# Splitting the projection weights of two mixers ahead of time, during the feed-forward layers

## The chip, the cores and the metric

The kernel runs on one core of a Trainium2 chip. The metric is the device time of one execution in microseconds (us). The engines are named as in the profile: PE is TensorE (matrix products), PEld its weight loads, DVE is VectorE, ACT is ScalarE, POOL is GpSimd, SP is SyncE, which issues all DMAs of this kernel.

## The reference

Two blocks of two layers each over 512 tokens of 1024 features; the first block has 256 context tokens besides. All in float32.

```python
# first block, layers l = 0, 1
xl = xl + g1 * mixer_l(modulate(xl, ...))           # l = 0: gated linear attention + chunk MLP; l = 1: MLA + DFT
xl = xl + g2 * conv_ffn(modulate(xl, ...))          # up to 2 x 2816, convolution over 3 tokens, down to 1024
# second block
h = rms_norm(x) * (1 + scale) + shift
qa, ka, va, qb, kb, vb, g = split(h @ ab_w_in)      # first mixer: 8 dilated heads, 4 differential heads
x = x + gate * ((concat(ya, yb) * silu(g)) @ ab_w_out)
q, k, v, g = split(h @ c_w_in)                      # second mixer: 16 heads, 4 of keys and values, a band of 128
x = x + gate * ((y * silu(g)) @ c_w_out)
return rms_norm(x) * final_g
```

The modulation vectors (scale, shift, gate and so on) are products of a vector with matrices `ada_w` and `ada_w_2`; those matrices are read from DRAM too.

## The kernel before

Every product in float32 is made of three matmuls in the faster type float32r: an operand x is split into a high part H (x rounded to float32r) and a low part L = x - H, and the product is H H + L H + H L. The activations are split when they are made. The weights lie in DRAM as float32, packed in the order of their use as blocks of 128 partitions x up to 1024 columns (512 KB); a block serves 128 output features over 1024 input features (24 matmuls over 512 tokens), or half of the inputs for 256 output columns.

`Stream` carries them. `load` issues the DMA of the next block into a tile `raw` (line 71; `SLOTS` = 5 slots, shared with the matrices of the modulation vectors, which are loaded in line 242). `prep` makes a block's parts:

```python
nc.scalar.activation(h[:, :n], src, AF.Copy)                                    # line 85: wH
nc.vector.tensor_tensor(l[:, :n], src, h[:, :n].bitcast(F32), op=ALU.subtract)  # line 86: wL
```

Its tiles wH and wL have `HL` = 4 buffers each, and once a block has been split, the next raw load is issued, so that three raw blocks are loaded ahead. `take` hands a block to the product and first prepares the block behind it (`AHEAD` = 1; at the end of an output product 2). The products are `lin` (by features) and `lin_tm` (by tokens); all matmuls go through `mm`, line 333 in the profile.

The modulation vectors are made in steps spread over the products: a step takes a raw tile of 512 KB, ScalarE multiplies it (lines 304 and 308) and GpSimd adds it up (line 309); only then is its raw slot free. `run` emits such a step each time the counted time of TensorE has advanced by a set pace (9.2 us in the feed-forward layers, 11 us in the first mixer of the second block). A step's load is emitted together with its use.

The feed-forward layers are `ffn(0, ...)`, over 768 tokens, and `ffn(1, ...)`, over 512: three groups of hidden blocks, each an up product `up` and a down product `dn`. The first mixer of the second block is `even2`: it makes the keys, queries (`ab_kq`, 16 blocks), values (`ab_va`, `ab_vb`, 8) and gates (`ab_g`, 8) of 8 units (a unit is two dilated heads or one differential head with two softmaxes), and attends unit by unit; the products of unit i + 1 are emitted behind the attention of unit i and fill TensorE between its steps. The second mixer `odd2` does the same with `c_k` (2 blocks), `c_v` (2), `c_q` (8) and `c_g` (8). The output products `ab_out` and `c_out` follow. A scheduler at compile time sets the order of instructions on each engine by priority (the order of emission) and by when tiles come free; each engine, and SyncE's queue of DMA issues, works through its list in order.

Of the kernel before, what the change touches and what calls it, by code (L numbers as in the profile page):

```python
# [13 lines left out]
F32 = mybir.dt.float32  # L14
F32R = mybir.dt.float32r
U8 = mybir.dt.uint8
AF = mybir.ActivationFunctionType
ALU = mybir.AluOpType
# [29 lines left out]
class Stream:  # L48
    """Weight blocks in the order of their use, loaded ahead and split into two float32r parts."""

    def __init__(self, kk):
        self.kk = kk
        self.groups = []
        self.blocks = []
        self.loaded = self.prepped = self.used = 0
        self.raw = {}
        self.ready = {}

    def add(self, tag, ap, widths):
        g = len(self.groups)  # L60
        self.groups.append((ap, sum(widths)))
        o = 0
# [4 lines left out]
    def load(self):  # L67
        if self.loaded < len(self.groups):
# [6 lines left out]
    def prep(self):  # L75
# [3 lines left out]
        tag, g, o, n, last = self.blocks[self.prepped]  # L79
        while self.loaded <= g:  # L80
            self.load()
# [10 lines left out]

    def ahead(self, n):
# [3 lines left out]
    def take(self, tag, ahead=None):  # L97
        """The next block's parts; the blocks behind it are made ready first."""
# [4 lines left out]
        self.ahead(self.kk.AHEAD if ahead is None else ahead)  # L103
# [3 lines left out]
class Banks:  # L107
    """A product's token runs, each in a bank of PSUM that is taken when it is first named."""
# [14 lines left out]
class Kern:  # L123
# [5 lines left out]
    GLA_POOL = True  # L129

# [35 lines left out]
    def psum(self, parts, **banks):  # L166
        """Who takes which of the banks, in turn, from here on; parts: who, by part of the tokens."""
# [16 lines left out]

    def setup(self):
# [3 lines left out]
        self.ps = self.open("ps", space=bass.MemoryType.PSUM)  # L189
        self.psum(("mm", "mm", "aux"), mm=(0, 2, 1, 3), aux=(4, 6, 5))  # L190
# [43 lines left out]
    def ada_load(self, pool=None, bufs=0):  # L234
        """Step (m, b, n, k, d): of vector m the blocks of 128 columns b .. b + n, of its matrix the rows k .. k + d."""
# [16 lines left out]
    def ada_put(self, m, b, n, value, nv):  # L252
        """The modulation vector's blocks b .. b + n have their product: value."""
# [15 lines left out]
    def ada_pe(self, n):  # L269
        """The next n steps of modulation vectors, by TensorE."""  # L270
# [19 lines left out]
    def ada(self):  # L290
        """The modulation vectors: sums over the chunks of the rows by GpSimd, over the partitions by TensorE."""
# [1725 lines left out]
```

## Time and profile before

| | |
|---|---|
| median of 3 runs | 2305.15 us (2303.86 to 2305.77) |
| span of the profiled execution | 2305.6 us |
| TensorE busy | 2199.9 us (95%) |
| VectorE busy | 1542.2 us (67%) |
| ScalarE busy | 1118.7 us (49%) |
| GpSimd busy | 407.4 us (18%) |

The profiled execution has no time of its own beside its span; the span is 0.45 us over the median of the runs. In the profiled execution the first feed-forward layer runs from about 489 to 1050 us, the second from 1385 to 1712, the first mixer of the second block from there to about 2040, its output product to about 2067, and the second mixer to the end.

A row of busy time counts an engine's instructions; a busy TensorE is not a TensorE at its peak. "Idle" of a stretch is its length less the busy time. PEclk is the granted clock of TensorE as a share of full speed.

### The profile page before, as it was taken

To read this page: it belongs to the slowest core of one execution; us is meant where nothing else is said; L and a number is where in the kernel's file an instruction comes from. 1 tells how busy PE (TensorE), PEld (TensorE's weight loads), DVE (VectorE), ACT (ScalarE), POOL (GpSimd) and SP (SyncE) were. 2 spreads that over 40 slices of the span, in tenths; PEclk is the share of its full clock that TensorE was granted. 3 is DMA by queue.
4 is the path that set the end of the run, shared out by engine and by line. 5 is a ranking of instruction groups with operands and counts; after the bars stand their busy time and mean duration, and the time that the engine had idled before them with its cause. 6 is when DMAs were issued, how large, how long until landed. Compare 5 with 4: busy or idle time off the path is not lost.

```text
span 2305.6 us, 34273 instructions
## 1 busy us (share of the span) xinstructions
PE 2199.9 (95%) x13243; PEld 1880.2 (82%) x13243; DVE 1542.2 (67%) x2938; ACT 1118.7 (49%) x2124; POOL 407.4 (18%) x389
## 2 busy tenths in 40 slices
PE   6899899989999999999999999999999989989997
PEld 4788798788888888888889878878788877778886
DVE  5867775486545544547798675454567867968996
ACT  5444443254423423334577454343446756746773
POOL 0323321012122221221000013222211122101110
PEclk9999999999999999999999999999999999989999
DMA  9111111713333334331220134445434232213111
GB/s 322 65 47 32 33 56 38 283 56 125 106 117 110 113 107 128 105 115 59 76 92 1 46 119 138 145 131 155 137 108 137 80 95 92 73 56 95 56 46 37
DMA packets 86708, 226.78 MB, mean 98 GB/s; under 512 B 7184, under 2 KB 15376, under 8 KB 86544
## 3 DMA queue, kind: packets, MB, share of 16 engines
q1 hardware_dynamic: 86544, 224.58, 30.6%
q8 instruction: 104, 1.70, 0.3%
q14 instruction: 60, 0.49, 0.1%
HBM read 222.46 MB, written 2.10 MB: 97 GB/s over the span
## 4 chain that ended last, share of the span: by engine, by line
PE 75%; DVE 15%; ACT 5%; issue 2%; DMA 2%; POOL 1%; SPq 0%; DVEq 0%; ACTq 0%; POOLq 0%
PE b L333 72%; DVE wL L86 2%; DMA raw<-in_ada_w_dram 2%; DVE hL L463 1%; DVE n_t L461 1%; PE b L1130 1%; ACT wH L85 1%; PE b L280 1%; DVE s L1139 1%; DVE ptL L386 1%; PE b L1018 1%; DVE ksL L1092 1%; DVE n_acc L478 0%; PE b L316 0%; ACT ptH L385 0%
## 5 line engine op out<-in xcount | busy, mean ns | idle before, releaser
L333 PE MATMUL b<-hH,wH 128*128 128x256 f32 (+1 forms) x1880 | 597.6, 359 | 15.3 <-ACT hH L462 8.0
L333 PE MATMUL b<-hH,wL 128*128 128x256 f32 (+1 forms) x1880 | 593.5, 357 | 3.6 <-DVE wL L86 3.6
L333 PE MATMUL b<-hL,wH 128*128 128x256 f32 (+1 forms) x1880 | 588.9, 356 | 2.9 <-DVE hL L463 2.8
L309 POOL TENSOR_TENSOR gacc<-gacc,raw 128x512 f32<-128x512 f32 x182 | 261.5, 1437 | 1002.6 <-ACT raw L308 971.5
L333 PEld LDWEIGHTS b<-hH,wH 128*128 128x128 f32 x1880 | 356.0, 191 | 70.6 <-ACT hH L462 9.6
L333 PEld LDWEIGHTS b<-hH,wL 128*128 128x128 f32 x1880 | 357.6, 191 | 52.8 <-DVE wL L86 4.2
L333 PEld LDWEIGHTS b<-hL,wH 128*128 128x128 f32 x1880 | 355.5, 191 | 53.7 <-DVE hL L463 3.9
L86 DVE TENSOR_TENSOR wL<-raw,wH 128x1024 fp32r<-128x1024 f32 (+2 forms) x270 | 341.9, 1268 | 73.9 <-ACT wH L85 73.2
L85 ACT ACTIVATE wH<-raw 128x1024 fp32r<-128x1024 f32 (+2 forms) x270 | 278.1, 1031 | 176.0 <-PE b L333 173.4
L308 ACT ACTIVATE raw<-raw,csil 128x512 f32<-128x512 f32 x182 | 125.6, 717 | 202.4 <-DMA raw<-in_ada_w_dram 134.1
L333 PE MATMUL b<-hidH,wH 128*128 128x512 f32 (+1 forms) x563 | 167.8, 345 | 0.0
L333 PE MATMUL b<-hidH,wL 128*128 128x512 f32 (+1 forms) x563 | 167.4, 344 | 0.0
L333 PE MATMUL b<-hidL,wH 128*128 128x512 f32 (+1 forms) x563 | 167.2, 344 | 0.0
L333 PE MATMUL b<-yH,wH 128*128 128x256 f32 (+1 forms) x408 | 129.5, 334 | 5.1 <-ACT yH L385 4.9
L333 PE MATMUL b<-yH,wL 128*128 128x256 f32 (+1 forms) x408 | 129.5, 333 | 1.5 <-DVE wL L86 1.5
L333 PE MATMUL b<-yL,wH 128*128 128x256 f32 (+1 forms) x408 | 129.5, 334 | 0.0
L668 DVE TENSOR_SCALAR a<-gp,vecs 128x769 f32<-128x769 f32 (+1 forms) x44 | 39.1, 888 | 123.9 <-ACT gp L664 123.9
L333 PEld LDWEIGHTS b<-hidH,wH 128*128 128x128 f32 x563 | 105.5, 188 | 14.5 <-issue 1.2
L333 PEld LDWEIGHTS b<-hidH,wL 128*128 128x128 f32 x563 | 105.8, 188 | 13.6
L333 PEld LDWEIGHTS b<-hidL,wH 128*128 128x128 f32 x563 | 105.8, 188 | 13.1
L385 ACT ACTIVATE ptH<-b 128x384 fp32r<-128x384 f32 (+2 forms) x160 | 77.7, 500 | 64.7 <-PE b L1130 49.0
L333 PE MATMUL b<-wH,hH 128*128 128x256 f32 x352 | 100.9, 288 | 2.7 <-ACT z L519 1.5
(366 smaller groups left out, 3938.9 us busy)
## 6 DMA issues: line engine op xcount, KB each, us to landing
raw<-in_weights_dram SPq DMA_DIRECT2D x231, 512.0 KB, 3.5
raw<-in_ada_w_dram SPq DMA_DIRECT2D x144, 512.0 KB, 3.9
raw<-in_weights_dram SPq DMA_DIRECT2D x32, 448.0 KB, 3.3
x0t<-in_xT_dram SPq DMA_DIRECT2D x4, 768.0 KB, 7.0
xlat<-in_xT_dram SPq DMA_DIRECT2D x2, 1024.0 KB, 10.2
out_dram<-fo SPq DMA_DIRECT2D x8, 256.0 KB, 2.3
raw<-in_weights_dram SPq DMA_DIRECT2D x3, 384.0 KB, 3.0
xctx<-in_xT_dram SPq DMA_DIRECT2D x2, 512.0 KB, 7.0
```

Source lines behind the costliest of these rows:

```text
L85: nc.scalar.activation(h[:, :n], src, AF.Copy)
L86: nc.vector.tensor_tensor(l[:, :n], src, h[:, :n].bitcast(F32), op=ALU.subtract)
L280: nc.tensor.matmul(acc[32 * q:32 * q + 32, :], self.csil[:, k + a, :], raw[:, a, :, q, :], start=k + a == 0, stop=k + a == KD - 1)
L308: nc.scalar.activation(raw[:, a], raw[:, a], AF.Copy, scale=c)
L309: nc.gpsimd.tensor_tensor(acc[v], acc[v], raw[:, a], op=ALU.add)
L333: self.nc.tensor.matmul(ps, lhsT, rhs, start=start, stop=stop, **kw)
L385: self.nc.scalar.activation(h, src, AF.Copy)
L386: self.nc.vector.tensor_tensor(l, src, h.bitcast(F32), op=ALU.subtract)
L461: nc.vector.scalar_tensor_tensor(t, x(j, s, e), A[:, j, v:v + 1], r, op0=ALU.mult, op1=ALU.mult)
L463: nc.vector.scalar_tensor_tensor(hL[j][:, s:e], t, b, h.bitcast(F32), op0=ALU.add, op1=ALU.subtract)
L668: nc.vector.tensor_scalar(a, gp[:, 1:1 + L], cw(1, i), cb(i), op0=ALU.mult, op1=ALU.add)
L1018: nc.tensor.transpose(ps[:, c], P[:, a, c], self.ident)
```

## The change

The 32 blocks of `ab_kq`, `ab_va`, `ab_vb`, `ab_g` (tags `EARLY_EVEN`) are loaded and split during `ffn(0)`, the 20 blocks of `c_k`, `c_v`, `c_q`, `c_g` (`EARLY_ODD`) during `ffn(1)`, by a generator `make` that `run` advances by one block each time TensorE's counted time has grown by 13 us. Both parts are written to tiles in DRAM. In the mixers `prep` then loads the two parts by two DMAs straight into wH and wL instead of loading raw and splitting; `load` passes over these blocks, so the raw slots go to the blocks behind them; and `take` asks for two blocks ahead instead of one when the next block is such a one. `make` has a pool of its own, `early` (two raw tiles, two H, one L), that is closed before the last down product. The output weights and all other weights are split as before. Comments and docstrings are dropped as well.

```diff
     def load(self):
+        while self.loaded < len(self.groups) and self.split_before(self.loaded):
+            self.loaded += 1
         if self.loaded < len(self.groups):
...
     def prep(self):
...
         tag, g, o, n, last = self.blocks[self.prepped]
+        if self.split_before(g):
+            pair = []
+            for name, src in zip(("wH", "wL"), self.made.pop(self.prepped)):
+                pair.append(ring.tile([128, 1024], F32R, name=name, tag=name, bufs=self.kk.HL))
+                nc.sync.dma_start(pair[-1][:, :n].bitcast(F32), src)
+            self.ready[self.prepped] = pair
+            self.prepped += 1
+            return
...
+    def split_before(self, g):
+        return self.tags[g] in self.kk.EARLY
+
+    def make(self, tags, sbuf, dram):
+        nc = self.kk.nc
+        todo = [(i, *b) for i, b in enumerate(self.blocks) if b[0] in tags]
+        raw = []
+
+        def load(k):
+            if k < len(todo):
+                i, tag, g, o, n, _ = todo[k]
+                raw.append(sbuf.tile([128, 1024], F32, name="er", tag="er", bufs=2))
+                nc.sync.dma_start(raw[-1][:, :n], self.groups[g][0])
+
+        load(0)
+        for k, (i, tag, g, o, n, _) in enumerate(todo):
+            load(k + 1)
+            src = raw.pop(0)[:, :n]
+            h = sbuf.tile([128, 1024], F32R, name="eH", tag="eH", bufs=2)[:, :n]
+            l = sbuf.tile([128, 1024], F32R, name="eL", tag="eL", bufs=1)[:, :n]
+            nc.scalar.activation(h, src, AF.Copy)
+            nc.vector.tensor_tensor(l, src, h.bitcast(F32), op=ALU.subtract)
+            self.made[i] = [dram.tile([128, n], F32, name="ed%s%d" % (p, i)) for p in "HL"]
+            for d, t in zip(self.made[i], (h, l)):
+                nc.sync.dma_start(d, t.bitcast(F32))
+            yield
...
     def take(self, tag, ahead=None):
...
-        self.ahead(self.kk.AHEAD if ahead is None else ahead)
+        n = self.kk.AHEAD if ahead is None else ahead
+        if self.used < len(self.blocks) and self.split_before(self.blocks[self.used][1]):
+            n = max(n, self.kk.AHEAD_EARLY)
+        self.ahead(n)
         return self.ready.pop(i)
...
+    AHEAD_EARLY = 2
+    EARLY_EVEN = ("ab_kq", "ab_va", "ab_vb", "ab_g")
+    EARLY_ODD = ("c_k", "c_v", "c_q", "c_g")
+    EARLY = EARLY_EVEN + EARLY_ODD
...
     def run(self, *gens):
...
+                while self.pe >= self.make_next:
+                    next(self.make_gen, None)
+                    self.make_next = self.pe + self.make_every
...
     def ffn(self, l, T, segs, parts, n, x, nxt, side):
...
         self.ada_pace(9.2)
+        self.make_gen = self.W.make((self.EARLY_EVEN, self.EARLY_ODD)[l], self.open("early", n.side), self.dram)
+        self.make_every = (13.0, 13.0)[l]
+        self.make_next = self.pe + 6.0
...
             if last:
+                for _ in self.make_gen:
+                    pass
+                self.make_next = math.inf
+                self.close("early")
                 self.close(n.name)
```

## Rows read from the trace of the kernel before

**Rows 1.** The page: busy time by engine, and GB/s in 40 slices.

```profile
PE 2199.9 (95%) x13243; PEld 1880.2 (82%) x13243; DVE 1542.2 (67%) x2938; ACT 1118.7 (49%) x2124; POOL 407.4 (18%) x389
...
GB/s 322 65 47 32 33 56 38 283 56 125 106 117 110 113 107 128 105 115 59 76 92 1 46 119 138 145 131 155 137 108 137 80 95 92 73 56 95 56 46 37
```

**Rows 2.** Windows by stage: us, busy by engine (instructions), PEclk, DMA share, GB/s.

```profile
489.00:1050.00 561.00, 555.11 (x3343) 486.96 (x3342) 298.87 (x378) 206.75 (x302) 130.04 (x93) 0.99 0.35 111
1385.00:1712.00 327.00, 326.45 (x1477) 262.63 (x1475) 170.05 (x201) 131.43 (x182) 80.35 (x53) 1.00 0.46 139
1712.00:1745.00 33.00, 29.44 (x230) 28.45 (x230) 29.58 (x65) 20.66 (x43) 5.12 (x4) 0.95 0.38 120
1745.00:2000.00 255.00, 242.95 (x1255) 195.26 (x1256) 201.79 (x432) 174.22 (x337) 47.47 (x32) 0.99 0.30 94
...
2063.00:2100.00 37.00, 36.18 (x270) 33.71 (x269) 33.85 (x73) 23.76 (x50) 5.86 (x8) 1.00 0.26 78
2100.00:2240.00 140.00, 139.66 (x729) 113.61 (x727) 128.68 (x402) 101.93 (x281) 19.75 (x38) 1.00 0.21 65
```

**Rows 3.** Timeline of TensorE, 1800 to 1950: start, us, instruction, [idle before, releaser].

```profile
1833.85 0.63 PE L1130 MATMUL b<-ident,P 128*128 128x128 f32 x4 [0.58 <-DVE P L1287]
...
1839.07 0.63 PE L1130 MATMUL b<-ident,P 128*128 128x128 f32 x4 [0.87 <-DVE P L1287]
...
1865.91 0.75 PE L333 MATMUL b<-ksH,qs 128*128 128x512 f32 x1 [3.23 <-DVE sm L1139]
...
1888.08 0.66 PE L1130 MATMUL b<-ident,P 128*128 128x128 f32 x4 [1.06 <-DVE ptL L386]
...
1918.44 0.50 PE L333 MATMUL b<-ksH,qs 128*128 128x512 f32 x1 [0.92 <-DVE sm L1139]
...
1920.97 0.63 PE L1130 MATMUL b<-ident,P 128*128 128x128 f32 x4 [0.83 <-DVE P L1287]
```

**Rows 4.** Chain of waits, 1840 to 1915, in order of time: start us, us, what.

```profile
1850.17 5.67 DMA raw<-in_ada_w_dram
...
1860.06 2.23 DVE wL L86
...
1886.20 1.23 DVE wL L86
...
1911.82 3.58 DMA raw<-in_ada_w_dram
```

**Rows 5.** Groups of lines, 1745 to 2000: busy us, mean ns, idle before.

```profile
L86 DVE TENSOR_TENSOR wL<-raw,wH 128x1024 fp32r<-128x1024 f32 x29 | 37.7, 1301 | 3.9 <-ACT wH L85 3.8
...
L85 ACT ACTIVATE wH<-raw 128x1024 fp32r<-128x1024 f32 x30 | 31.5, 1051 | 0.6 <-PE b L333 0.5
```

**Rows 6.** Waits, 1745 to 2000: us in total, times, longest.

```profile
SPq L242 <- DVE wL L86: 94.7, 11, 26.7
...
ACT raw L308 <- DMA raw<-in_ada_w_dram: 10.4, 7, 3.3
```

**Rows 7.** Modulation matrices' loads, 1745 to 2000.

```profile
L242 SPq DMA_DIRECT2D raw<-in_ada_w_dram x16: 378/378/385, 1750.9 to 1977.8; - x16
...
DMA to landing us min/median/max: 3.5/3.7/5.7
```

**Rows 8.** Waits in the first feed-forward stretch, then in the second.

```profile
ACT wH L85 <- PE b L333: 45.6, 16, 7.3
...
PE b L333 <- DVE wL L86: 3.3, 1, 3.3
...
ACT wH L85 <- PE b L333: 76.8, 36, 4.4
```

**Rows 9.** Timeline of VectorE at the first boundary: start, us, instruction, [idle before].

```profile
1715.13 1.22 DVE L86 TENSOR_TENSOR wL<-raw,wH 128x1024 fp32r<-128x1024 f32 x1 [0.61 <-ACT wH L85]
```

**Rows 10.** Timeline of ScalarE and TensorE at the second boundary.

```profile
2063.50 1.05 ACT L85 ACTIVATE wH<-raw 128x1024 fp32r<-128x1024 f32 x1
...
2068.72 0.28 PE L333 MATMUL b<-hH,wH 128*128 128x256 f32 x1
```

More of the change, by code (lines that the diff above doesn't have):

```diff
@@ L53, in __init__ @@
         self.groups = []
+        self.tags = []
         self.blocks = []
@@ L57, in __init__ @@
         self.ready = {}
+        self.made = {}
     def add(self, tag, ap, widths):
@@ L61, in add @@
         self.groups.append((ap, sum(widths)))
+        self.tags.append(tag)
         o = 0
@@ L189, in setup @@
         self.ps = self.open("ps", space=bass.MemoryType.PSUM)
+        self.dram = self.open("dram", space=bass.MemoryType.DRAM)
+        self.make_gen, self.make_next = iter(()), math.inf
         self.psum(("mm", "mm", "aux"), mm=(0, 2, 1, 3), aux=(4, 6, 5))
@@ L463, in after @@
                 nc.vector.scalar_tensor_tensor(hL[j][:, s:e], t, b, h.bitcast(F32), op0=ALU.add, op1=ALU.subtract)
-        return SimpleNamespace(add=add, after=after, hH=hH, hL=hL, name=name, H=hHt)
+        return SimpleNamespace(add=add, after=after, hH=hH, hL=hL, name=name, side=side, H=hHt)
     def sumsq(self, pool, T, x):
```

## Prediction

> **What bounds the kernel now.** I read the page's busy line first, then the stretches by stage, then the gaps of TensorE inside the one stage where it has any to speak of, then the chain of waits and the waits of SyncE's queue there. The page shows TensorE busy 95% of the span, with VectorE at 67% and ScalarE at 49% [rows 1]: work taken from VectorE gains only where TensorE stands still for it. By stage [rows 2]: in the two feed-forward stretches TensorE is busy 555.1 of 561 us and 326.5 of 327 us, with VectorE at 53% and 52%. In the units of the second block's second mixer (2100 to 2240) it is busy 139.7 of 140, although VectorE is busy 92% there. The first mixer's stretch from 1745 to 2000 is another case: 243.0 of 255, so 12.05 us idle, with a granted clock of 0.99. So the place where these splits can cost time is that stretch, and little else: 1712 to 1745 has 3.6 us idle, 2063 to 2100 has 0.8. From 2000 on the first mixer ends with the last unit's own softmax and with output weights, which are still split in place.
>
> What ends the gaps between 1745 and 2000: six of them [rows 3] add up to 0.58 + 0.87 + 3.23 + 1.06 + 0.92 + 0.83 = 7.5 us, each released by VectorE. The chain of waits says what VectorE was late with [rows 4]: before the 3.23 us gap a modulation load was issued when a wL had freed its slot, ScalarE's multiplication of that load came 5.7 us later, and then two wL in a row (2.23 us) stood ahead of the statistics that release the score bank; before the 1.06 us gap stands one wL of 1.23 us. The waits show the same coupling in sum: SyncE's modulation loads waited 94.7 us for wL, and ScalarE, which works in order, stood 10.4 us in 7 waits for those loads [rows 6].
>
> **The change, part by part.**
>
> *Removed.* 52 splits: 16 + 8 + 8 blocks of the first mixer, 20 of the second. One costs 1301 ns on VectorE and 1051 ns on ScalarE [rows 5], together 68 and 55 us, which all move into the feed-forward layers. In 1745 to 2000 it is 29 wL (37.7 us of 201.8 busy) and 30 wH (31.5 of 174.2). What this buys on the path is bounded by nothing below (another link of the same chains takes the gap over) and by the whole 12.05 us above. I take the six gaps, 7.5 us, since before the two largest a wL is the link, and before the gap of 0.92 and the next a modulation load that came late [rows 4]. The clock: 0.99 over 255 us is about 2.6 us lost after pauses; I take half, 1.3.
>
> *Coupling of the loads.* Raw slots are no longer freed by wL: three stay with output weights that wait, two serve the modulation loads, freed by GpSimd's last addition. At one step per about 16 us (16 loads in that stretch [rows 7]) a load can be issued a step early, so ScalarE's 10.4 us of waits [rows 6] go. Their worth is inside the 7.5 us.
>
> *First boundary, 1712 to 1745.* The wL of 1.22 us at 1715.13 stands in VectorE's queue between the norm's steps [rows 9]; its block now comes by DMA. Two more follow in the norm's second half, while TensorE works. I take 1.0 us of gain; bounds 0 and the 3.6 us idle there.
>
> *Second boundary, 2063 to 2100.* The second of the first two key blocks gets its buffers when TensorE frees them at about 2063.5; today ScalarE then splits it at once, and the first matmul that needs it starts at 2068.72 [rows 10]. Now two loads of 512 KB run there. A load of 512 KB lands in 3.7 us [rows 7]; the second can land right behind the first or, at worst, a whole landing later, so the pair is there between 2067.2 and 2070.9: 0 to 2.2 us late. I take 0.5. The later key, value, query and gate blocks are asked for two ahead, which is at least one block of 48 half-width or 24 full-width matmuls before use: nothing.
>
> *Units of the second mixer, 2100 to 2240.* TensorE has 0.34 us idle: 0, though VectorE loses some 20 us of work. Tail from 2240: 0, its weights are unchanged.
>
> *Added in the feed-forward layers.* 32 and 20 times: one load, one ScalarE copy (1.05 us), one VectorE subtraction (about 1.2 to 1.3 us), two stores of 512 KB. VectorE goes from 298.9 to about 340 of 561 us and from 170.1 to about 196 of 327; ScalarE from 206.8 to 240 and from 131.4 to 152: room in sum [rows 2]. The cover is the depth of the weight preparation: ScalarE's wH waited for TensorE to free a buffer for 45.6 us in 16 waits in the first layer and 76.8 us in 36 in the second [rows 8], so it runs ahead of TensorE by all buffers there are, and a copy of 1.05 us or a wait behind it is absorbed. Without that cover each of the 52 would cost up to 2.3 us. It did fail in the first layer: TensorE stood 3.3 us for one wL [rows 8]. I take half of one more such stall, 1.5 us; bounds 0 and 6 (the first layer's waits, 5.9 us idle, once more). On SyncE's queue the two stores wait for ScalarE and VectorE, and the weight loads behind them wait along; three blocks are loaded ahead, so a wait of some us is hidden. Traffic in the second layer: 20 x 3 x 0.524 MB = 31.5 MB over 327 us are 96 GB/s on top of 139, so 235; the first slice of the page moved 322 [rows 1], so there is room, with longer landings. A store's landing is waited for by nobody until hundreds of us later.
>
> *Sum.* 2305.6 (span) - 7.5 - 1.3 - 1.0 + 0.5 + 1.5 = 2297.8. The profiled span lies 0.45 us above the median of the runs shown, 2305.15, so 2297.4.
>
> **A rule weighed.** The queue of SyncE is what the change lengthens: today its modulation loads already stood 94.7 us behind wL in 11 waits [rows 6]. The Trainium skill, "DMA: Bandwidth & Descriptors", section "Anatomy of one DMA", says that the DMA engines do not wait on semaphores; the wait is the issuing sequencer's, before it dispatches. By that rule a load of parts that waits for TensorE to free a wH buffer would hold every later load on the queue, and the trace agrees as far as SyncE's long waits go. What that would do here is the slower rival below.
>
> **The rivals.**
>
> *More is gained.* If the whole idle time of 1712 to 2000 goes (3.6 + 12.05), with 2.6 us of clock and no cost elsewhere: 2305.6 - 18.2 - 0.45 = 2287. For it: the second mixer's units keep TensorE at 139.7 of 140 us with VectorE at 92%, so VectorE at 64% (201.8 - 37.7 of 255) need not leave gaps. Against: the first mixer's chains are longer (a norm per unit, a second softmax).
>
> *The gaps only move.* ScalarE, the transposes' split and the softmax take over as the last link, so that 4 us are left of the gains, and the 2.0 us of costs (feed-forward layers and second boundary) stay: 2305.6 - 4 + 2.0 - 0.45 = 2303, up to no change. For it: five of the six gaps are released by the weighting of P or by the score statistics [rows 3], which stay on VectorE.
>
> *SyncE's queue holds ScalarE.* A load of parts stands at the head, waiting for TensorE to free a wH or wL, with a modulation load behind it; ScalarE, in order, waits for that load, and the softmax behind it. The place is 1745 to 2000, the price of one such case is the gap that the same chain makes today, 3.23 us. It decides from two on: 2305.6 + 2 x 3.23 + 2.0 (feed-forward and second boundary) - 1.0 - 0.45 = 2312.6. Against it: two slots let a modulation load go a step early, so the head must be held for more than some 12 us (16 less a landing of 3.7 [rows 7]).
>
> **How the numbers follow.** About 0.2% (4.6 us) is what a measurement of this kernel can tell from no change, so faster is below 2300.5 and slower above 2309.8. The forecast, 2290 to 2300, has 0.50; more gained 0.17; the gaps only move 0.20; the queue 0.13. That is faster 0.67, same 0.20, slower 0.13. The range for 8 in 10 takes the larger gain as far as 2285 and, on the other side, the moved gaps, no change and the milder cases of the queue up to 2308; the faster cases alone lie in 2285 to 2300.
>
> **What would show it.** After the change, TensorE's idle time in the first mixer's units should fall from 12 to about 4 us, with no wL on VectorE there, no wait of SyncE's modulation loads for wL, and ScalarE's waits for them near zero. The feed-forward stretches should keep their lengths within 1.5 us, with wH still waiting for TensorE. The second mixer's units should keep their length. The prediction is wrong if TensorE waits for DMAs into wH or wL by more than a few us in sum, if the feed-forward stretches grow, or if ScalarE's waits for modulation loads grow in place of vanishing.

## The result, and the profile after

The changed kernel takes 2339.8 us (median of 4 runs, 2335.9 to 2342.3) beside 2305.5 us for the kernel before: a ratio of 1.0142, 95% interval 1.0128 to 1.0157. The forecast was 2297.4 us, with a range up to 2308. The profiled execution of after is 2334.1 us long, 28.5 more than that of before; it is the fastest of the four runs, and the medians lie 34.4 us apart, so the stages below account for 28.5 of these.

Every trace here holds 13243 matmuls, so a stage can be cut by counting them (numbers 3497, 6913, 8463, 10226, 11982 and 12909 open the stages below; the last stage is taken up to the last matmul). Lengths of stages in us, worked out so from the two traces:

```
                             before    after   difference
first feed-forward layer      570.3    592.3    +22.0
its neighbour, second mixer   275.2    274.9     -0.3
second feed-forward layer     385.8    402.3    +16.5
2nd block: first mixer, out   349.1    337.7    -11.4
2nd block: second mixer       167.8    168.6     +0.8
output product, end            58.9     60.2     +1.3
```

The second block is 9.3 us shorter. The feed-forward layers, which were to keep their lengths, are 38.5 us longer. One cut is not quite the same in both kernels: around number 10226 the small matmuls that sum a modulation vector stand at other places in the order. Cut at the first product of the mixer instead, the second layer is 17.9 us longer and the second block 10.7 us shorter.

Line numbers differ between the runs, since each is that of the run's own kernel. First the page of after, its busy line and its traffic in 40 slices (compare [rows 1]):

```profile
PE 2203.3 (94%) x13243; PEld 1877.9 (80%) x13243; DVE 1547.7 (66%) x2938; ACT 1120.4 (48%) x2124; POOL 411.8 (18%) x389
...
GB/s 319 64 46 37 28 55 64 262 102 289 295 279 277 198 121 126 105 122 57 74 102 1 42 169 281 301 269 156 136 162 244 133 133 167 64 118 148 109 64 37
```

The busy times are those of before, within 6 us. The traffic is not: it stands at about 270 to 300 GB/s in slices 10 to 13 and 25 to 27 and then falls back, to between 105 and 160 for most of the rest of the layers. The last store of a block made ahead lands 295 us after the start of the first layer and 219 us after that of the second; the blocks are not spread over the layers. The waits of after in the first layer (488 to 1080), then in the second (1356 to 1759), from the views of waits (us in total, times, longest):

```profile
ACT raw L359 <- DMA raw<-in_ada_w_dram: 101.3, 22, 7.5
ACT eH L128 <- DMA er<-in_weights_dram: 58.7, 22, 8.2
DVE eL L129 <- DMA edL<-eL: 44.6, 15, 8.7
...
ACT wH L98 <- PE b L384: 20.9, 9, 5.5
...
ACT wH L98 <- PE b L384: 49.8, 23, 4.3
ACT raw L359 <- DMA raw<-in_ada_w_dram: 36.3, 17, 5.0
ACT eH L128 <- DMA er<-in_weights_dram: 30.4, 14, 6.5
DVE eL L129 <- DMA edL<-eL: 24.3, 9, 5.9
```

ScalarE stands 89 us for raw blocks that are to be split, VectorE 69 us for the store of the one eL buffer to land. ScalarE's waits for modulation loads are no longer than before in the first layer (101.3 beside 103.2 us in before) and longer in the second (36.3 beside 20.6). The slack of ScalarE ahead of TensorE, 45.6 and 76.8 us in [rows 8], is down to 20.9 and 49.8. The timeline of TensorE in after has seven gaps of 1.9 us or more among the products of the two layers that before does not have, and an eighth at the norm behind them; six of the seven (start, us, instruction, [idle before, releaser]):

```profile
620.01 1.28 PE L384 MATMUL b<-hH,wH 128*128 128x256 f32 x2 [2.81 <-ACT gp L718]
...
653.47 1.01 PE L384 MATMUL b<-hidL,wH 128*128 128x256 f32 x2 [5.21 <-DVE hidL L437]
...
727.48 0.35 PE L384 MATMUL b<-hH,wH 128*128 128x256 f32 x1 [2.53 <-DVE xctx L747]
...
1444.41 0.66 PE L367 MATMUL b<-gacc,ones 128*32 128x128 f32 x8 [3.36 <-ACT gp L718]
...
1492.39 0.47 PE L384 MATMUL b<-hidH,wH 128*128 128x512 f32 x1 [1.92 <-DVE gacc L369]
...
1538.72 0.66 PE L367 MATMUL b<-gacc,ones 128*32 128x128 f32 x8 [6.18 <-POOL gacc L360]
```

None waits for weights. TensorE waits for evacuations (gp, xctx), for hidden tiles (hidL) and for modulation sums (gacc): work that stands on ScalarE and VectorE behind something late. What was late ahead of the first two gaps is in the timelines of ScalarE and VectorE:

```profile
618.63 1.06 ACT L128 ACTIVATE eH<-er 128x1024 fp32r<-128x1024 f32 x1 [1.95 <-DMA er<-in_weights_dram]
619.60 0.85 ACT L718 ACTIVATE gp<-b 128x256 f32<-128x256 f32 x2
...
649.60 0.75 DVE L357 SCALAR_TENSOR_TENSOR gacc<-raw,csil,gacc 128x512 f32<-128x512 f32 x1 [4.89 <-DMA raw<-in_ada_w_dram]
```

At 620 us ScalarE had stood for a raw block, split it and only then evacuated gp. At 653 us VectorE had stood 4.89 us for a modulation load and made a wL before the hidL that TensorE needed. Ahead of the last gap, the timeline of SyncE's queue, ScalarE and GpSimd shows one modulation load and who waits for it:

```profile
1531.61 0.38 SPq L293 DMA_DIRECT2D raw<-in_ada_w_dram  x1
...
1536.00 0.72 ACT L355 ACTIVATE gacc<-raw,csil 128x512 f32<-128x512 f32 x1 [3.81 <-DMA raw<-in_ada_w_dram]
...
1537.41 1.28 POOL L360 TENSOR_TENSOR gacc<-gacc,raw 128x512 f32<-128x512 f32 x1 [5.83 <-ACT raw L359]
```

The granted clock falls at five of the seven gaps. Windows of after ahead of the first two gaps, right behind the second, and later (PE busy first, then PEld, DVE, ACT, POOL; PEclk, DMA share, GB/s):

```profile
545.00:600.00 55.00, 55.00 (x330) 48.19 (x330) 37.27 (x41) 28.38 (x38) 14.82 (x10) 1.00 0.87 292
```

```profile
653.50:657.50 4.00, 4.00 (x13) 3.42 (x14) 3.07 (x5) 2.17 (x3) 1.38 (x1) 0.50 0.71 253
658.00:700.00 42.00, 42.00 (x255) 36.68 (x254) 24.86 (x28) 14.29 (x17) 9.70 (x7) 1.00 0.83 294
```

At 292 GB/s TensorE runs without a pause at the full clock, and its matmuls keep the same 0.04 us behind those of before from 545 to 615 us, so traffic by itself does not slow matmuls here. The two gaps, 2.81 + 5.21 us, delay the matmuls around them by 5.0 + 8.2 us against before. Most of the difference is the clock: behind the second gap it is 0.50 of full speed, the lower of its two levels (1.2 GHz in place of 2.4), and 1.00 again from 658 us on. At the gaps of 727 and 1492 us (2.53 and 1.92 us) it stayed at 1.00, and the second of these delays the matmuls by 2.2 us only.

### The profile page after: what moved, and what is told of

Same layout as the page of the kernel before. It is cut to its first block, busy times and chain, and to the rows that moved or that the text cites. A ratio compares the mean times of both kernels' runs of the same rounds, so it can differ in the third digit from the quotient of the medians.

```text
span 2334.1 us, 34624 instructions
## 1 busy us (share of the span) xinstructions
PE 2203.3 (94%) x13243; PEld 1877.9 (80%) x13243; DVE 1547.7 (66%) x2938; ACT 1120.4 (48%) x2124; POOL 411.8 (18%) x389
## 4 chain that ended last, share of the span: by engine, by line
PE 61%; DVE 14%; DMA 10%; ACT 6%; issue 6%; POOL 3%; SPq 0%; DVEq 0%; ACTq 0%; POOLq 0%
PE b L384 58%; DMA raw<-in_ada_w_dram 5%; DMA edL<-eL 3%; DVE wL L99 2%; POOL gacc L360 2%; DMA er<-in_weights_dram 2%; DVE n_t L515 1%; PE b L1191 1%; DVE hL L517 1%; ACT wH L98 1%; ACT raw L359 1%; PE b L331 1%; PE b L1079 1%; DVE eL L129 0%; ACT P L1201 0%
## 5 line engine op out<-in xcount | busy, mean ns | idle before, releaser
L384 PE MATMUL b<-hH,wH 128*128 128x256 f32 (+1 forms) x1880 | 602.1, 361 | 26.3 <-ACT hH L516 10.7
L99 DVE TENSOR_TENSOR wL<-raw,wH 128x1024 fp32r<-128x1024 f32 (+4 forms) x218 | 276.2, 1269 | 76.9 <-ACT wH L98 76.5
L98 ACT ACTIVATE wH<-raw 128x1024 fp32r<-128x1024 f32 (+4 forms) x218 | 223.1, 1025 | 118.1 <-PE b L384 115.3
L129 DVE TENSOR_TENSOR eL<-er,eH 128x1024 fp32r<-128x1024 f32 x52 | 69.5, 1337 | 74.7 <-DMA edL<-eL 68.9
L437 DVE TENSOR_TENSOR ptL<-b,ptH 128x384 fp32r<-128x384 f32 (+2 forms) x160 | 89.0, 565 | 27.0 <-ACT ptH L436 25.5
```

Of the source, the lines that this page charges most:

```text
L129: nc.vector.tensor_tensor(l, src, h.bitcast(F32), op=ALU.subtract)
L384: self.nc.tensor.matmul(ps, lhsT, rhs, start=start, stop=stop, **kw)
L437: self.nc.vector.tensor_tensor(l, src, h.bitcast(F32), op=ALU.subtract)
```

## The experiments

Differences of stage lengths from before, in us, cut as above (columns: first feed-forward layer; second; second block's first mixer and output; the rest of that block), and the timed ratio to before on the same chip, with its interval. A stage comes from one profiled execution and scatters by some us; the ratio decides.

```
                 ffn 1   ffn 2   mixer   rest   ratio
after            +22.0   +16.5   -11.4   +2.1   1.0142 (1.0128 to 1.0157)
gain_alone        +4.5    +3.2    -8.5   +2.4   0.9974 (0.9960 to 0.9988)
cost_alone       +25.3   +18.1    -2.0   +0.2   1.0172 (1.0149 to 1.0195)
traffic_only     +14.9   +14.5    -7.6   +2.3   1.0099 (1.0074 to 1.0124)
no_stores        +17.0   +10.8    -8.8   +2.5   1.0102 (1.0081 to 1.0123)
paced            +13.2   +14.7   -11.6   +2.7   1.0090 (1.0064 to 1.0117)
after_late       +25.2   +20.5   -16.3   +2.2   1.0142 (1.0127 to 1.0157)
late              +9.7    +9.8   -17.4   +2.5   1.0021 (1.0008 to 1.0034)
gain_late         +1.2    +4.2   -16.0   +2.2   0.9976 (0.9965 to 0.9986)
before_late       +2.5    +1.0    -0.3   +0.1   1.0006 (0.9996 to 1.0015)
actq             +18.8   +21.4    -7.7   +2.5   1.0146 (1.0130 to 1.0163)
late_actq        +17.5   +13.2   -16.6   +2.3   1.0080 (1.0062 to 1.0098)
late_pre          +9.0    +3.6   -17.7   +2.2   1.0014 (1.0003 to 1.0026)
late_slow        +15.8    +5.2   -17.3   +2.2   1.0058 (1.0038 to 1.0077)
even_plain       +11.7   +17.7    -8.6   -0.2   1.0106 (1.0092 to 1.0119)
even_slow        +12.7    +3.0   -19.2    0.0   1.0020 (1.0009 to 1.0032)
even_late         +0.9    +8.8   -15.6   +0.2   0.9989 (0.9978 to 0.9999)
even_late13       +0.6    +5.2   -17.5   +0.1   0.9974 (0.9961 to 0.9986)
```

In the forms with the order edit (*late* below) eight modulation matmuls more fall into the mixer, so the cut by count moves. Cut at the first product of the mixer, the second layer and the mixer read +17.9 and -12.8 in after, +4.0 and -9.3 in gain_alone, +7.5 and -15.1 in late, +1.9 and -13.8 in gain_late, -1.3 and +2.0 in before_late, +3.0 and -15.2 in even_late13: up to some 3 us of these two columns hang on the cut.

**Gain and cost apart.** *gain_alone*:

```diff
+        every, todo = todo, todo[:1]
...
+            for j, *_ in every:
+                self.made[j] = self.made[i]
```

> Leaves out all but the first of the splits made ahead in each feed-forward layer; the 52 blocks of the second block load that one pair of parts again and again, so the loads of parts keep their size, number and place, and the output is that of other weights. Theory (the whole loss lies in the feed-forward layers and the second block alone gains 11.7 us): 2305.5 - 11.7 = 2294, between 2291 and 2297, feed-forward layers 570 and 385 us long as before. Rival (the second block is only shorter because work was pushed out of it into the longer feed-forward layers, modulation steps above all): 2300 to 2306.

*cost_alone*:

```diff
-        return self.tags[g] in self.kk.EARLY
+        return False
```

> The splits ahead are made and stored as in the change, but nothing reads them: the second block loads raw blocks and splits them in place as before. Theory (the loss is that of making them, and comes whether they are used or not): 2305.5 + 40 = 2345, between 2340 and 2350, feed-forward layers 592 and 403 us long. Rival (part of the loss comes from the loads behind: the weight stream skips the early groups, so that its ring holds other blocks in the feed-forward layers): 2325 to 2338.

The cost comes whether the parts are used or not (1.0172; median 2350.0, at the upper end of what was expected). The gain alone is 0.26%, some 6 us beside that chip's 2309.5, about half of the 11.7 expected and inside the rival's range; the second block is 6.1 us shorter here beside 9.3 in after. (Most of the +4.5 us of its first layer is one wait at the start of the layer, 5.74 us for the norm's hL at 516 us, 1.59 us in before; why stays open. The profiled execution is 4.8 us slower than the median.)

What the rival names can be counted. The loads of modulation matrices in the second layer, in before and then in after:

```profile
L242 SPq DMA_DIRECT2D raw<-in_ada_w_dram x34: 378/379/379, 1344.2 to 1712.1; - x34
```

```profile
L293 SPq DMA_DIRECT2D raw<-in_ada_w_dram x38: 367/379/480, 1366.0 to 1753.0; - x38
```

Every form that loads parts in the mixers has 38 to 40 there, and 10 to 12 in the first mixer; before, before_late and cost_alone, which load none, have 34 and 16. So modulation work did move out of the mixer into the second layer. It has a price at the layer's end, where TensorE waits for the sums of squares of the norm (n_acc). Before, then ScalarE (n_sq are the squares) and TensorE in after:

```profile
1712.36 0.70 PE L333 MATMUL b<-n_acc,ones 128*128 128x256 f32 x2 [0.91 <-DVE n_acc L478]
```

```profile
1749.49 1.33 ACT L359 ACTIVATE raw<-raw,csil 128x512 f32<-128x512 f32 x2 [1.38 <-DMA raw<-in_ada_w_dram]
1750.72 0.40 ACT L531 ACTIVATE n_sq<-xlat 128x256 f32<-128x256 f32 x1
...
1751.94 0.70 PE L384 MATMUL b<-n_acc,ones 128*128 128x256 f32 x2 [2.96 <-DVE n_acc L532]
```

The wait is 0.9 us in before, before_late and cost_alone and 2.1 to 4.2 us in every form that loads parts, gain_alone (3.30) and gain_late (3.16) among them. This part of the loss is not that of making parts.

**Traffic or work.** *traffic_only* stores the raw tile twice, from three raw buffers in place of two:

```diff
-                raw.append(sbuf.tile([128, 1024], F32, name="er", tag="er", bufs=2))
+                raw.append(sbuf.tile([128, 1024], F32, name="er", tag="er", bufs=3))
...
-            nc.scalar.activation(h, src, AF.Copy)
-            nc.vector.tensor_tensor(l, src, h.bitcast(F32), op=ALU.subtract)
...
-            for d, t in zip(self.made[i], (h, l)):
-                nc.sync.dma_start(d, t.bitcast(F32))
+            for d, t in zip(self.made[i], (src, src)):
+                nc.sync.dma_start(d, t)
```

> Keeps every load and both stores of the 52 blocks, but takes the copy off ScalarE and the subtraction off VectorE: the raw block is stored twice, so the low part is wrong. Theory (the in-order engines stand for the loads and stores of the blocks, 89 us on ScalarE and 69 us on VectorE by the waits, and TensorE behind them): most of the 40 us goes, 2294 to 2304, feed-forward layers at most 8 us longer than before together. Rival 1 (the traffic itself, 280 to 300 GB/s, makes weights and modulation rows late): 2325 to 2340. Rival 2 (only the engines' work of 2.3 us a block costs): 2292 to 2296, no trace of the traffic at all.

*no_stores*:

```diff
-            for d, t in zip(self.made[i], (h, l)):
-                nc.sync.dma_start(d, t.bitcast(F32))
+            if k == 0:
+                pair = [dram.tile([128, n], F32, name="ed%s%d" % (p, i)) for p in "HL"]
+                for d, t in zip(pair, (h, l)):
+                    nc.sync.dma_start(d, t.bitcast(F32))
+            self.made[i] = pair
```

> The change as it was, unpaced, but only the first block of each layer is stored; the others are loaded and split and dropped, and the second block loads that one pair each time, so the output is that of other weights. Engine work is that of the change, extra bytes in the feed-forward layers a third of it. Theory (what is waited for is DMA: landings of the raw block on ScalarE, of the store on VectorE, of the modulation rows): of 22.0 and 18.2 us at least half goes, 576 to 582 and 389 to 395, ratio 0.999 to 1.005. Rival (engine work of 2.3 us a block): 588 to 592 and 400 to 403, ratio 1.012 to 1.015.

Both theories fell as sole causes. Without any split, 29.4 of 38.5 us stay; without two thirds of the extra bytes, 27.8 stay. The two add up to more than the whole. That fits a TensorE that stands only for the last of several late things, each kind of delay being enough; no run shows this by itself. Where TensorE stands differs. The timeline of traffic_only has the modulation sum in the second layer; that of no_stores the evacuation behind ScalarE's copies:

```profile
1530.00 0.66 PE L363 MATMUL b<-gacc,ones 128*32 128x128 f32 x8 [6.43 <-POOL gacc L356]
```

```profile
1443.11 0.66 PE L369 MATMUL b<-gacc,ones 128*32 128x128 f32 x8 [7.14 <-ACT gp L720]
```

How long modulation loads take beside this traffic is in the views of their lines, in the second layer of before (137 GB/s) and then in after, 1400 to 1571 (284 GB/s):

```profile
DMA to landing us min/median/max: 3.5/3.7/5.4
```

```profile
DMA to landing us min/median/max: 4.3/5.7/7.8
```

In the first layer the median goes from 3.8 to 4.3 us only.

**Pace and order.** *paced* ties each load and each copy to real progress:

```diff
+        def pace(t):
+            if self.kk.pace is not None:
+                nc.vector.tensor_scalar(t[:, :1], self.kk.pace, 1.0, None, op0=ALU.mult)
...
+                pace(raw[-1])
...
+            pace(h)
...
+                    self.pace = hf[:, :1]
...
+                    self.pace = x(b, s, e)[:, :1]
```

> The change, with two tiny VectorE operations more per block: one element column of the raw buffer and one of the high part's buffer is first written from the newest hidden or residual tile, so that neither the load nor the copy can run ahead of the feed-forward layer's own progress; the real values overwrite them. Theory (the loss comes from running ahead: all blocks are made in the first 300 us of 570 and 170 us of 385, in a burst of DMA on whose landings ScalarE and VectorE stand): feed-forward layers within 4 us of 570 and 385, total 2294 to 2302, below the kernel before. Rival (the work costs what it costs, 52 times a copy and a subtraction on engines that release TensorE): 2330 to 2340 whatever the pace.

The forecast of the theory failed (1.009), though most of the waits it spoke of went. The view of waits of paced, first layer (44.6 and 58.7 us in after):

```profile
DVE eL L135 <- DMA edL<-eL: 13.5, 4, 4.6
ACT eH L134 <- DMA er<-in_weights_dram: 5.5, 2, 5.2
```

and what TensorE stands for in its second layer:

```profile
1435.27 0.43 PE L373 MATMUL b<-gacc,ones 128*32 128x128 f32 x8 [3.64 <-ACT gp L724]
...
1658.60 0.65 PE L373 MATMUL b<-gacc,ones 128*32 128x128 f32 x8 [6.88 <-POOL gacc L366]
```

ScalarE's slack ahead of TensorE is back at 43.7 us in the first layer (20.9 in after, 45.6 in before). So a second theory: the modulation chain (load, ScalarE, GpSimd) runs behind its place in the order, and TensorE meets it there. *late* is paced with the sums 5 us later in TensorE's order; *after_late* and *before_late* have this edit alone on the two kernels, *gain_late* on gain_alone:

```diff
             if k + d == KD:
+                yield "late"
                 nv = len(acc)
...
-                    next(self.ada_gen, None)
-                    self.ada_next = self.pe + self.ada_every
+                    due = self.pe + self.ada_every - self.ada_lag
+                    self.ada_lag = 5.0 if next(self.ada_gen, None) == "late" else 0.0
+                    self.ada_next = self.pe + self.ada_lag if self.ada_lag else due
```

> The paced form, and the small matmuls that sum a finished modulation vector over the partitions stand 5 us of TensorE's time later in the order than its last addition. Theory 1 (the rest of the loss comes from modulation loads that land late, so that TensorE, in order, stands for GpSimd's last addition: 3.64 and 6.88 us in the second layer, 13 us with what follows each): second layer 386 to 391 us in place of 400.5, first layer about as paced, 583; ratio to before 1.002 to 1.005. Theory 2 (it is not that wait but bytes or engine work everywhere): second layer stays at 398 to 402, ratio 1.008 to 1.010.

> The change as it was, unpaced, with the small matmuls of a finished modulation vector 5 us later in TensorE's order. If the late modulation vectors were the whole loss: ratio to before 1.001 to 1.004, as paced and later together. If running ahead is a cost of its own (ScalarE and VectorE standing for the landings of raw blocks and stores, 5.0 and 8.2 us of delay near 620 to 670 us, which no matmul of a modulation vector stands in): 1.005 to 1.010.

> The kernel before with nothing but the later matmuls: the control. It has no wait of TensorE for a modulation vector in the feed-forward layers, so the edit should give nothing there: ratio 0.998 to 1.001. If it gives 0.996 or less, part of what the paced and later form won was won by the edit and not for the change.

> Only the first block of each layer made, all loads of parts kept (output of other weights), with the later matmuls. This is what the change would be worth if making the parts cost nothing. Theory (no cost in the feed-forward layers, second block 8 to 17 us shorter): ratio 0.991 to 0.996, feed-forward layers 570 to 575 and 385 to 389 us. Rival (the shorter second block of the paced and later form, 331.8 us, came from modulation steps done in its longer feed-forward layers): 0.996 to 0.999.

The pair of edits takes 1.0142 to 1.0021. Pace alone gives 1.009, order alone nothing (1.0142), which is above both ranges expected of it: unpaced, the waits only change places, as the timeline of after_late shows:

```profile
1539.82 0.43 PE L369 MATMUL b<-gacc,ones 128*32 128x128 f32 x8 [3.02 <-POOL gacc L361]
...
1591.72 0.66 PE L369 MATMUL b<-gacc,ones 128*32 128x128 f32 x8 [4.06 <-ACT gp L721]
```

The ratio of late is in theory 1's range; its second layer, 395.7 us, lies between the ranges of the two theories. The control before_late is no faster (1.0006). gain_late, 0.9976, is within the rival's range, above what the theory gave: all that this change was worth with the cost of making parts taken away is about 0.25%. The gap that late keeps is again ScalarE in order, behind a modulation load; its timeline, then the windows behind it:

```profile
1007.36 1.33 ACT L366 ACTIVATE raw<-raw,csil 128x512 f32<-128x512 f32 x2 [3.36 <-DMA raw<-in_ada_w_dram]
...
1009.44 0.83 ACT L444 ACTIVATE hidH<-hf 128x768 fp32r<-128x768 f32 x1
...
1010.32 1.01 PE L392 MATMUL b<-hidH,wH 128*128 128x256 f32 x2 [4.76 <-ACT hidH L444]
```

```profile
1010.00:1015.50 5.50, 4.46 (x13) 3.46 (x14) 4.83 (x7) 2.02 (x4) 0.82 (x1) 0.50 0.54 171
1016.00:1035.00 19.00, 19.00 (x111) 16.73 (x110) 7.50 (x10) 6.12 (x10) 6.14 (x4) 1.00 0.28 91
```

A gap of 4.76 us costs 8.1 us against the same matmuls of before: the granted clock is at its lower level, 0.50, up to 1015.50 and at 1.00 from 1016 on.

**SyncE's queue.** *actq*, and *late_actq* with the order edit (the blocks are made in half steps of 6.5 us, with a third one-column write each):

```diff
-                nc.sync.dma_start(raw[-1][:, :n], self.groups[g][0])
+                nc.scalar.dma_start(t[:, :n], self.groups[g][0])
...
+            yield
+            pace(l, l[:, :1].bitcast(F32))
...
-                nc.sync.dma_start(d, t.bitcast(F32))
+                nc.scalar.dma_start(d, t.bitcast(F32))
```

> The paced form with the loads and stores of the blocks that are made on ScalarE's DMA queue in place of SyncE's, the stores half a step behind the subtraction. Bytes and engine work stay. Theory 1 (SyncE's queue, in order, stands for the copy, the subtraction and the pace operations, about 95 us more in the first layer, and holds modulation and weight loads behind): first layer 570 to 576, second 385 to 391, ratio 0.996 to 1.001. Theory 2 (the DMA engines are shared, and loads land 0.5 to 1.2 us later whatever queue they come from): 580 to 584 and 397 to 401, ratio 1.007 to 1.010, with ScalarE's waits for modulation loads as long as in the paced form (144 and 78 us).

> Both edits together. If each cures what its theory says: 570 to 574 and 384 to 388, ratio 0.995 to 0.999, below the kernel before. If the bytes cost it whatever the order: not below 1.004.

This theory fell: 1.0146 and 1.0080, slower by 0.6% than the same forms on SyncE's queue. The waits for modulation loads are as long as before the move; in the first layer of actq they are

```profile
ACT raw L376 <- DMA raw<-in_ada_w_dram: 94.3, 21, 10.1
...
DVE gacc L374 <- DMA raw<-in_ada_w_dram: 38.9, 15, 5.8
ACT gacc L372 <- DMA raw<-in_ada_w_dram: 37.5, 8, 9.7
```

which is 171 us, beside 166 in paced. It was 172 in the kernel before, though, so this sum does not tell the forms apart. What made actq slower than paced was not settled; the half steps and the third write are not told apart from the queue.

**Loads ahead, spacing, number.** *late_pre* loads one modulation step ahead, *late_slow* spaces its blocks by 16.0 and 17.5 us:

```diff
+            if self.ada_loaded <= self.ada_used:
+                self.ada_load()
             if k + d == KD:
```

> The paced and later form, with each modulation load issued one step (9.2 us of TensorE's time) ahead of its use. Theory (what is late is the modulation load, issued when its step comes and landing 4 to 5 us after, with ScalarE in order behind it, 135 us of such waits in the first layer): those waits fall below 60 us, the last large gap (4.76 us, ScalarE's copy of the hidden tile) goes, feed-forward layers 570 to 576 and 385 to 391 us, ratio 0.994 to 1.000. Rival (the load ahead takes a slot from the weight blocks, and weights come late in its place): 1.002 to 1.008.

> The paced form with later matmuls and loads ahead, blocks spaced 16.0 and 17.5 us in place of 13. Theory (the cost goes with the rate at which blocks are made): the gap of 3.58 us before the last product of the first layer may stay, the rest of the 8 us goes, first layer 572 to 577, second 386 to 389, ratio 0.997 to 1.000. Rival (each block costs the same however spread): ratio 1.001 to 1.003.

Neither did what it was for. In late_pre ScalarE still stands 122 us for modulation loads in the first layer (112 in late), and the ratio differs from that of late by less than the intervals; the wider spacing was slower (1.0058), with 7.77 us of idle TensorE at the same place, 1018 us, where blocks were still being made. The control, *before_late_pre*, is the kernel before with these loads and the order edit:

> The kernel before with the later matmuls and the modulation loads one step ahead, nothing else: the control for the form above. Theory (the edits only undo harm done by the change): ratio 0.998 to 1.001. Rival (modulation loads ahead help the second block by themselves, its modulation loads being one of the links of the gaps there): 0.995 to 0.997.

It is itself slower, 1.0034 (1.0020 to 1.0048), where the order edit alone gave 1.0006: the loads ahead cost by themselves.

The *even* forms make only the first mixer's 32 blocks, half in each layer:

```diff
-    EARLY = EARLY_EVEN + EARLY_ODD
+    EARLY = EARLY_EVEN
...
-        self.make_gen = self.W.make((self.EARLY_EVEN, self.EARLY_ODD)[l], ...
+        self.make_gen = self.W.make((self.EARLY_EVEN[:1], self.EARLY_EVEN[1:])[l], ...
```

> The change as it was, unpaced, but without the 20 blocks of the second mixer; of the first mixer's 32 blocks, those of the keys and queries are made in the first layer and the others in the second. Theory (running ahead costs in proportion to the blocks made: 22.0/32 = 0.69 and 16.5/20 = 0.83 us each): 16 blocks in each layer cost 11 and 13 us, the second mixer and the tail give back 2.1: ratio 1.005 to 1.009. Rival (the burst itself costs, whatever its length): 1.010 to 1.013.

> Only the first mixer's 32 blocks, half in each layer, paced at 28 and 19 us, with later matmuls and loads ahead. Theory (the first mixer earns all the gain and widely spaced steps cost next to nothing): feed-forward layers 571 to 574 and 386 to 389, second block 14 to 17 us shorter, total 9 to 13 us below the kernel before, ratio 0.994 to 0.997. Rival (the steps keep a cost of their own, or the second mixer's blocks did earn): 0.998 to 1.001.

> Only the first mixer's 32 blocks, half made in each layer, paced, spaced 22 and 19 us, with later matmuls of the modulation vectors and no loads ahead. Theory (a made block costs nothing when it is held to real progress, no modulation matmul waits behind it, and all are done before the burst of modulation steps at 1005 us): feed-forward layers 570 to 574 and 386 to 390, second block 16 to 19 us shorter, ratio 0.995 to 0.998. Rival (two stores and a load more every 20 us still make modulation loads late): 0.999 to 1.003.

> The same with a spacing of 13 us. Theory as above (spacing does not matter once the order is right): within 0.001 of the other form. Rival (the rate of traffic decides): 0.002 to 0.004 above it.

even_plain: half of the blocks cost half in the first layer (11.7 of 22.0), but 16 in place of 20 cost no less in the second, so the cost is not one price per block. The second mixer's blocks earned nothing: without them the rest of the block is back at its old length, 2 us shorter. even_slow, which has the loads ahead, missed its ranges (1.0020), its first layer 12.7 us longer. **even_late13 beats both kernels**: 0.9974, 2298.6 us beside 2304.2, as much as gain_late showed to be there. The wider spacing of even_late was not better (0.9989, intervals overlap); even_late13 was expected within 0.001 of it or above, and neither came. The windows of even_late13 over the two layers:

```profile
487.00:1058.00 571.00, 564.16 (x3420) 495.24 (x3419) 335.51 (x442) 229.15 (x330) 127.91 (x93) 1.00 0.46 153
1333.00:1725.00 392.00, 381.13 (x1773) 309.19 (x1772) 240.04 (x320) 180.87 (x259) 100.78 (x71) 0.99 0.62 209
```

TensorE is busy 564 of 571 us with 16 blocks made beside it. In the second layer its products start when those of before do (1700.18 us beside 1700.24 for the same matmul near the end); the +5.2 us lie behind that, at the norm (a wait of 3.15 us for n_acc), with 40 modulation loads in the layer. So the making of 32 blocks costs nothing that these traces show, once it is paced and the sums stand later; what is left is the modulation work that moved.

## Why the prediction was wrong

**The step that failed** is "Added in the feed-forward layers": 1.5 us, bounds 0 and 6, measured 38.5 (39.9 by the other cut; some 2 us of it are the wait for n_acc). It is also the sign that the prediction named itself, feed-forward stretches that grow. Three things in it were wrong.

*The cover.* The step named the depth of the weight preparation, ScalarE's wH waiting for TensorE [rows 8]. That covers weights, and no weight was later than before. The same two engines also evacuate PSUM, make the hidden tiles and feed the modulation sums, which have no such depth; a wait behind a copy reaches TensorE through those, as at 620 us. The price without cover, "up to 2.3 us" for each of 52, counted engine time only; the waits for landings (89 and 69 us) were not in it. "A store's landing is waited for by nobody" was wrong: eL has one buffer, and the next subtraction waits for its store.

*The pace.* The blocks are emitted one per 13 us, and the sum took them as spread so: 235 GB/s in the second layer. In the trace they run ahead, at 270 to 300 GB/s, with ScalarE and VectorE waiting for the buffers' landings. Paced against unpaced, with the order edit in both, is 1.0021 against 1.0142: shown.

*The modulation chain.* The prediction saw it in the second block only. In the layers its loads land later (median 3.7 to 5.7 us in the second layer's burst, 3.8 to 4.3 in the first layer) and it falls behind its place in TensorE's order. Late against paced, 1.0021 against 1.0090: shown. Which part of the delay of those loads is sharing of the DMA engines and which is queueing stays open; moving the new DMAs off SyncE's queue did not help.

**The gain**, 9.3 us forecast (7.5 + 1.3 + 1.0 - 0.5), is 9.3 us in after by stage. That the numbers agree is luck: the other cut gives 10.7, and the terms are others. The windows of before from matmul 10226 to 11834, in three parts, then the same parts in after:

```profile
1719.60:1861.80 142.20, 137.86 (x804) 117.32 (x805) 116.36 (x256) 95.84 (x194) 24.02 (x16) 0.99 0.33 104
1861.80:1994.60 132.80, 122.74 (x606) 96.46 (x605) 103.99 (x224) 89.49 (x172) 25.91 (x16) 0.97 0.28 88
1994.60:2050.30 55.70, 48.17 (x205) 36.44 (x206) 39.28 (x76) 25.65 (x47) 0.00 (x0) 0.88 0.14 46
```

```profile
1757.80:1905.30 147.50, 139.33 (x807) 118.73 (x806) 100.39 (x238) 81.86 (x181) 26.62 (x18) 0.99 0.51 182
1905.30:2028.60 123.30, 118.17 (x605) 94.84 (x605) 89.21 (x211) 71.55 (x147) 14.34 (x9) 1.00 0.35 123
2028.60:2076.90 48.30, 43.23 (x203) 32.85 (x202) 35.55 (x72) 26.06 (x48) 0.00 (x0) 1.00 0.10 31
```

Idle time of TensorE in the last two windows falls from 10.1 + 7.5 to 5.1 + 5.1 us, 7.4 in sum, and its busy time for the same matmuls from 170.9 to 161.4, with the clock at 1.00 in place of 0.97 and 0.88: 9.5 us, where the term of the clock was 1.3 and "from 2000 on" was put at nothing. Over all three windows idle time falls by 3.6 us (21.9 to 18.4), where 7.5 + 1.0 were forecast.

The first boundary was forecast 1.0 us shorter. Matmul for matmul, after lies 37.4 us behind before at 1740 us and 43.1 at 1780: 5.7 us longer. TensorE stands there for n_acc (2.96 us, 0.91 in before), for the norm's hH (2.58 and 0.89 us, once 1.85 in before) and hL (1.86 us), with 182 GB/s moved in the window in place of 104. With the order edit the waits for hL and the second for hH are gone from this place in late and even_late13, the one for n_acc is not; the mixer is then 16 to 19 us shorter by count, 13 to 17 from its first product. The second mixer was put at 0.5 us longer, at its start, and lost 0.8; the end was put at 0 and lost 1.3.

One reading of [rows 4] was wrong: the 2.23 us were not two wL in a row but one, which took 2.32 us (VectorE's timeline, 1859.97). The sum does not use it. It does take 0.45 us off the span to come to the timed median; in after the profiled execution's own time lies 1.8 us above its span (2335.9 and 2334.1), so that step had no basis beyond the one kernel.

**The rivals.** The queue rival had its mechanism and not its price. In 1785 to 2040 of after, in the views of waits:

```profile
SPq L89 <- PE b L384: 143.0, 31, 9.8
```

```profile
ACT raw L359 <- DMA raw<-in_ada_w_dram: 8.3, 5, 2.7
```

A load of parts does hold the queue for TensorE, 143 us in all; ScalarE behind it waits 8.3 us, less than the 10.4 of [rows 6]. That such a wait stands on the sequencer that issues is what the Trainium skill, "DMA: Bandwidth & Descriptors", section "Anatomy of one DMA", says; the section describes GpSimd's path, and this trace agrees for SyncE's, with the 143 us above. That the gaps only move did happen, but in the feed-forward layers. No rival had those layers as its place.

## What to carry to other kernels

Work that is moved to a place where an engine has room in sum must be priced by what stands behind it on that engine, in order, and by the landings it waits for; ask what each engine releases there, not only how busy it is. An emission order is no pace: buffers and data set when a step really runs, and a tiny dependence on a fresh result can hold it back. Move only what earns something: 20 of the 52 blocks bought nothing. And look where the work goes that a change sets free: here modulation steps came early and stood ahead of a norm.

## What the runs showed of the hardware

A pause of TensorE of 4.76 us cost 8.1 us: the granted clock was 0.50, the lower level (1.2 GHz), from 1010 to 1015.5 us and 1.00 from 1016 us on. Two pauses of 8.0 us together cost 13.2; one of 1.92 us, with the clock at 1.00 throughout, cost 2.2. Loads of 512 KB landed in 3.7 us (median) at 137 GB/s and in 5.7 us (up to 7.8) at 284 GB/s, while TensorE ran at full clock and 55.00 of 55 us at 292 GB/s. SyncE's queue head waited 143 us in 31 pieces in the first mixer, and ScalarE's waits for the loads behind it got no longer.
